# GpSimd takes one weight piece and half of a subtraction behind each norm, and the feed-forward's last transposes move between held products

## The chip, the cores and the metric

The kernel runs on one core of one Trainium2 chip. The metric is the device time of one execution in microseconds (us). The core has TensorE (PE, matrix products), VectorE (DVE, elementwise work), ScalarE (ACT, activations and copies), GpSimd (POOL, here elementwise work and loads of rows) and SyncE (SP, whose queue issues the weight loads). Each engine works its own instruction queue in order, and waits on semaphores of the others.

## The reference: what is computed

A first block (three token mixers and a mixture of experts) feeds a second block of four transformer layers over 256 tokens of width 1024. The change lies in the second block:

```python
def layer_norm(x, g, b):
    mu = xf.mean(-1, keepdims=True)
    var = jnp.square(xf - mu).mean(-1, keepdims=True)
    return (xf - mu) * lax.rsqrt(var + LN_EPS) * g + b

def swiglu(x, w_gate_up, w_down):
    gate, up = split(x @ w_gate_up)            # D_FF = 2816 each
    return (silu(gate) * up) @ w_down

for i in range(4):                             # attention kinds A, B, C, A
    h = mixer(x)
    x = layer_norm(DN_ALPHA * x + h, ln_g[i, 0], ln_b[i, 0])
    x = layer_norm(DN_ALPHA * x + swiglu(x, w_gate_up[i], w_down[i]), ln_g[i, 1], ln_b[i, 1])
```

All values are float32.

## The kernel before, in words

**Products.** Each float32 matrix is split into a high part (a cast to the type that PE reads, L240 for weights, L218 for activations, on ACT) and a low remainder (L242 and L219, a subtraction on DVE). A product is three matrix instructions: high x high, high x low, low x high (L254, L255, L256 in `mm3_steps`; L264, L265, L262 in `mm3_part`). The 256 tokens are two halves of 128 (t = 0, 1).

**Weight pieces.** `stream` cuts a weight matrix into pieces of 128x1024, two row blocks of 128 each; a projection over 1024 rows takes four of them. `unit` loads one piece (SP, into one of four raw buffers), casts it on ACT and subtracts on DVE, which frees the raw buffer for the next load. The split pair goes into one of three buffers of its own or, where `pair` names one, into one of four buffers that the attention heads use otherwise (`flat_heads`).

**Norms.** After each of the eight sublayers `finish` runs: the residual of half 0 (L1993 or L1995 with the statistics L1996), `normalise` of half 0, its transposes on PE (`turn`, L370) and the split of these (L218, L219), then the same for half 1. `normalise` takes mean and variance (L2011), the reciprocal root in seven steps on 128x1 (`rsqrt`, L326 to L341), the two halves of 512 columns of (y - mean) * g (L2014) and the two halves of y * r + b (L2016). All of it runs on DVE. The row vectors g and b are loaded by DMAs that POOL issues (L400).

**Behind a norm.** The first projection that follows (of the attention in `project_at` with `first`, of the feed-forward in `ffn` at u = 0) takes its four pieces as one group: all products of half 0, the high parts first, then `rest`, which turns half 1, then those of half 1. So PE has the work of half 0 while half 1 is normalised.

**End of the feed-forward.** `ffn` runs eleven steps of 256 hidden columns: gate and up products, SwiGLU (L2101 on ACT, L2103 on DVE), four transposes (L2117), their split, and one step later the down products into four accumulators, acc[t][n]. In the last step (u = 10) the down products of step 9 for half 0 are held back (`held`: two pieces, for n = 0 and n = 1, twelve products), then come the transposes of step 10, then the products of step 10 for half 0 (`last`), then all 24 of half 1, under which half 0 is normalised.

**What sets the order.** The kernel is traced in program order; a planner then orders each engine's queue by simulated times, and `after(ins)` keeps what it encloses behind `ins` on that engine. `self.order` carries the order of PE through the last products.

Of the kernel before, what the change touches and what calls it, by code (L numbers as in the profile page):

```python
# [9 lines left out]
F32 = mybir.dt.float32  # L10
# [4 lines left out]
ALU = mybir.AluOpType  # L15
AX = mybir.AxisListType
ACT, DVE, PE = mybir.EngineType.Activation, mybir.EngineType.DVE, mybir.EngineType.PE
P = 128
D = 1024
KT = D // P  # L20
D_FF = 2816
# [11 lines left out]
ONE, ALL = (1, 1, 1, 1), (4,)  # L33

# [115 lines left out]
class Core:  # L150


    def __init__(self, tc, I, ctx):
# [11 lines left out]
        self.behind = self.behind_act = None  # L165
# [61 lines left out]
    def unit(self, srcs, nk, pair=None, raw=None):  # L227


        nc = self.nc  # L230
        n = sum(x.shape[2] for x in srcs)
        view = lambda t: t[:, : nk * n].rearrange("p (k n) -> p k n", k=nk)
        raw = self.raw() if raw is None else raw
        h, l = self.split_pair() if pair is None else pair
        at = 0
        for x in srcs:
            nc.sync.dma_start(view(raw)[:, :, at : at + x.shape[2]], x)
            at += x.shape[2]
        with self.after(self.behind_act if pair is None else None):
            nc.scalar.copy(h[:, : nk * n], raw[:, : nk * n])  # L240
        with self.after(self.behind if pair is None else None):
            nc.vector.tensor_sub(l[:, : nk * n], raw[:, : nk * n], h[:, : nk * n].bitcast(F32))  # L242
        return view(h), view(l)
# [23 lines left out]
    def stream(self, w, cols, nk=KT, pair=lambda: None):  # L267

        v = w.rearrange("(k p) n -> p k n", p=P)
        for k in range(0, nk, 2):  # L270
            yield self.unit([v[:, k : k + 2, c : c + n] for c, n in cols], 2, pair())
# [1340 lines left out]
class Block2:  # L1612
# [52 lines left out]
    def project_at(self, first, xT, w, cols, pss):  # L1665

        c = self.c
        if first:
            pairs = chain([None] * self.first_pairs, (self.flat_heads() for _ in count()))
            self.first_pairs = 0  # L1670
            c.project(xT, c.stream(w, cols, pair=lambda: next(pairs)), pss, groups=ALL if self.rest else ONE, rest=self.rest)
# [334 lines left out]
    def normalise(self, y, st, rows):  # L2006
# [6 lines left out]
        for sl in HALVES:  # L2013
            nc.vector.scalar_tensor_tensor(y[:, sl], y[:, sl], mv[:, 0:1], rows[0][:, sl], ALU.subtract, ALU.mult)  # L2014
# [47 lines left out]
    def ffn(self, xT, i, x, more):  # L2062
# [19 lines left out]
        def add_all(t, ks):  # L2082

            for n in range(2):
# [6 lines left out]
        for u in range(nu):  # L2091
            pss = [c.mm() for _ in range(2)]
            units = c.stream(wg, [(256 * u, 256), (D_FF + 256 * u, 256)], pair=self.flat_heads)
# [11 lines left out]
            if u == nu - 1:  # L2105
                self.order = c.last(PE)
                held = list(pieces(*pend, lambda: next(pairs)))
                add_all(0, held)
# [6 lines left out]
            for kk in range(2):  # L2115
                for t in range(2):
                    nc.tensor.transpose(ps[:, kk * 256 + t * P : kk * 256 + (t + 1) * P], av[t][:, kk * P : (kk + 1) * P], c.ident)  # L2117
# [73 lines left out]
```

## Time and profile before

| | us |
|---|---|
| median of three runs (2033.51 to 2035.86) | 2034.7 |
| the profiled execution | 2037.31 |
| its span, first to last instruction | 2035.5 |
| PE busy | 1931.8 |
| DVE busy | 1336.6 |
| ACT busy | 1035.3 |
| POOL busy | 135.9 |

PE's granted clock over the span was 0.973 of full speed. Busy time is the union of an engine's instructions. In a timeline row, the bracket behind an instruction gives the idle time of its engine before it and what ended that. A row with x4 merges four like instructions that follow each other. Starts are in us from the span's start; the line is that of the kernel before.

### The profile page before, as it was taken

How to read it: one execution, taken by the hardware profiler on the slowest of the kernel's cores; microseconds unless marked ns; L12 is line 12 of the kernel's file. 1: busy time of each engine (PE TensorE's matmuls, PEld its weight loads, DVE VectorE, ACT ScalarE, POOL GpSimd, SP SyncE). 2: the span in 40 equal slices, each digit the busy share in tenths (PEclk: the TensorE clock that was granted, in tenths of full speed). 3: DMA queues.
4: the chain of work that ended last, by engine and by line, in shares of the span. 5: the costliest groups of instructions: out<-in, count | busy, mean ns of one | idle time of the engine just before them, and what ended most of it. 6: DMA issues, size and time to landing. Idle time of an engine off the chain costs nothing.

```text
span 2035.5 us, 27804 instructions
## 1 busy us (share of the span) xinstructions
PE 1931.8 (95%) x10012; PEld 1546.8 (76%) x10012; DVE 1336.6 (66%) x2324; ACT 1035.3 (51%) x1656; POOL 135.9 (7%) x259
## 2 busy tenths in 40 slices
PE   6998998989998999999999999999999999999997
PEld 2886886867786678887888877887767888767886
DVE  4689887868897775556555466556566555867555
ACT  5555654546774744434655555443563444454442
POOL 2110000000002000002111200000110000300000
PEclk8999998989998899999999999999999999989999
DMA  9546644777995356654543456664554655435662
GB/s 310 162 140 194 183 139 147 236 247 245 321 323 162 116 166 199 186 176 131 170 136 110 147 178 202 191 186 145 156 176 129 201 187 176 155 104 175 188 189 80
DMA packets 272403, 364.61 MB, mean 179 GB/s; under 512 B 17018, under 2 KB 206677, under 8 KB 272256
## 3 DMA queue, kind: packets, MB, share of 16 engines
q1 hardware_dynamic: 264832, 338.38, 52.5%
q0 software_dynamic: 7424, 24.36, 3.8%
q8 instruction: 81, 1.33, 0.3%
q14 instruction: 66, 0.54, 0.1%
HBM read 359.53 MB, written 3.15 MB: 178 GB/s over the span
## 4 chain that ended last, share of the span: by engine, by line
PE 59%; DVE 6%; ACT 2%; DMA 1%; issue 1%; POOL 0%; SPq 0%; DVEq 0%; ACTq 0%; POOLq 0%
PE mm L254 14%; PE mm L255 13%; PE mm L256 13%; PE acc L254 4%; PE acc L256 4%; PE acc L255 4%; PE acc L1752 1%; PE acc L1650 1%; DVE arena L242 1%; PE acc L1929 1%; PE acc L2117 1%; ACT arena L240 1%; DVE arena L2014 1%; PE acc L1749 1%; DMA arena<-in_w_gate_up 1%; PE acc L1925 1%
## 5 line engine op out<-in xcount | busy, mean ns | idle before, releaser
L242 DVE TENSOR_TENSOR arena<-arena,arena 128x1024 fp32r<-128x1024 f32 x597 | 716.9, 1213 | 480.6 <-ACT arena L240 475.8
L240 ACT CAST arena<-arena 128x1024 fp32r<-128x1024 f32 x597 | 614.0, 1039 | 549.4 <-PE mm L256 298.9
L254 PE MATMUL mm<-arena 128*128 128x512 f32 (+1 forms) x1856 | 703.3, 385 | 12.7 <-ACT arena L240 6.8
L255 PE MATMUL mm<-arena 128*128 128x512 f32 (+1 forms) x1856 | 706.0, 381 | 0.3 <-DVE arena L242 0.3
L256 PE MATMUL mm<-arena 128*128 128x512 f32 (+1 forms) x1856 | 698.7, 380 | 3.5 <-DVE arena L1386 1.3
L254 PEld LDWEIGHTS mm<-arena 128*128 128x128 f32 x1856 | 352.9, 191 | 85.8 <-ACT arena L240 8.3
L256 PEld LDWEIGHTS mm<-arena 128*128 128x128 f32 x1856 | 352.3, 191 | 71.2 <-DVE arena L219 4.1
L255 PEld LDWEIGHTS mm<-arena 128*128 128x128 f32 x1856 | 354.0, 191 | 61.5 <-issue 1.8
L254 PE MATMUL acc<-arena 128*128 128x512 f32 (+5 forms) x736 | 235.5, 360 | 7.3 <-ACT arena L218 7.3
L255 PE MATMUL acc<-arena 128*128 128x512 f32 (+5 forms) x736 | 235.4, 351 | 0.5 <-DVE arena L219 0.5
L256 PE MATMUL acc<-arena 128*128 128x512 f32 (+4 forms) x736 | 231.8, 350 | 0.0
L218 ACT CAST arena<-acc 128x512 fp32r<-128x512 f32 (+2 forms) x174 | 92.7, 542 | 179.1 <-PE acc L2117 79.8
L219 DVE TENSOR_TENSOR arena<-acc,arena 128x512 fp32r<-128x512 f32 (+2 forms) x174 | 108.1, 632 | 99.1 <-ACT arena L218 98.7
L254 PEld LDWEIGHTS acc<-arena 128*128 128x128 f32 (+1 forms) x736 | 125.0, 190 | 40.3 <-issue 11.6
L255 PEld LDWEIGHTS acc<-arena 128*128 128x128 f32 (+1 forms) x736 | 125.7, 190 | 21.6 <-issue 1.8
L256 PEld LDWEIGHTS acc<-arena 128*128 128x128 f32 (+1 forms) x736 | 124.7, 190 | 20.5 <-DVE arena L219 1.7
L1685 ACT ACTIVATE arena<-arena,nm 128x128 f32<-128x128 f32 (+2 forms) x128 | 65.9, 517 | 27.1 <-DVE nm L1684 27.1
L768 DVE SCALAR_TENSOR_TENSOR arena<-arena 128x192 f32<-128x192 f32 (+1 forms) x160 | 64.9, 430 | 2.4 <-ACT arena L766 0.9
L1684 DVE CUSTOM_DVE_ANT_0 arena<-acc,arena 128x128 f32<-128x128 f32 (+2 forms) x128 | 53.1, 465 | 13.6 <-PE acc L256 13.6
L370 PE MATMUL acc<-arena 128*128 128x128 f32 x200 | 32.9, 302 | 24.1 <-DVE arena L1020 8.2
L370 PEld LDWEIGHTS acc<-arena 128*128 128x128 f32 x200 | 24.4, 153 | 34.8 <-DVE arena L1020 8.3
L2101 ACT ACTIVATE arena<-mm 128x256 f32<-128x256 f32 x88 | 32.4, 379 | 24.4 <-PE mm L256 11.9
(354 smaller groups left out, 1497.8 us busy)
## 6 DMA issues: line engine op xcount, KB each, us to landing
arena<-in_w_gate_up SPq DMA_DIRECT2D x352, 256.0 KB, 4.0
arena<-in_w_down SPq DMA_DIRECT2D x88, 512.0 KB, 3.6
arena<-in_b_w_qkv SPq DMA_DIRECT2D x144, 256.0 KB, 3.0
arena<-in_w_in SPq DMA_DIRECT2D x56, 512.0 KB, 4.0
arena<-in_ada_w SPq DMA_DIRECT2D x48, 512.0 KB, 5.7
arena<-in_moe_w_gate SPq DMA_DIRECT2D x64, 256.0 KB, 4.6
arena<-in_moe_w_up SPq DMA_DIRECT2D x64, 256.0 KB, 4.9
arena<-in_moe_w_down SPq DMA_DIRECT2D x32, 512.0 KB, 5.3
```

What stands on the lines that cost most here:

```text
L218: self.nc.scalar.copy(h, src)
L219: self.nc.vector.tensor_sub(l, src, h.bitcast(F32))
L240: nc.scalar.copy(h[:, : nk * n], raw[:, : nk * n])
L242: nc.vector.tensor_sub(l[:, : nk * n], raw[:, : nk * n], h[:, : nk * n].bitcast(F32))
L254: yield t.matmul(out, x[0], w[0], start=start, stop=False)
L255: yield t.matmul(out, x[0], w[1], start=False, stop=False)
L256: yield t.matmul(out, x[1], w[0], start=False, stop=stop)
L370: self.nc.tensor.transpose(ps[:, j * P : (j + 1) * P], src[:, j * P : (j + 1) * P], self.ident)
L768: nc.vector.scalar_tensor_tensor(ov[:, rows], x, w, ov[:, rows], ALU.mult, ALU.add)
L1684: nc.vector.tensor_tensor_reduce(pr, s, mask, -0.125, 3e38 if sink is None else sink, ALU.add, ALU.min, nm)
L1685: nc.scalar.activation(pr, pr, AF.Exp, bias=nm, scale=-1.0, accum_out=l)
L2101: nc.scalar.activation(s, ps[:, :256], AF.Silu)
```

## The change

In `unit`, pieces marked `pool` are copied and subtracted by POOL, with no order imposed; `stream` marks those whose number stands in `pool`. The first projection of each attention (`project_at`) and of each feed-forward (u = 0) marks piece 3, the fourth. In `normalise` the second half of (y - mean) * g becomes two POOL instructions, a subtraction with one value for each partition and a multiplication; the first half stays on DVE, which also keeps both last steps. In `ffn`, at the last step, the held products for n = 0 come first, then the transposes, then those for n = 1. The unused `behind_act` goes.

```diff
--- before.py
+++ after.py
@@ -31,6 +31,8 @@
 RAW, PAIRS, MM, PROBS, AHEAD = 4, 3, 3, 8, 2
 HALVES = slice(0, 512), slice(512, 1024)
 ONE, ALL = (1, 1, 1, 1), (4,)
+
+POOLED = (3,)
 
 
 def _parts_of_two_pi():
@@ -162,7 +164,7 @@
             t = self.const.tile([P, words], dt, name=f"arena{len(self.arenas)}")
             self.arenas[dt] = Arena(t, words, kept)
         self.raw(), self.split_pair()
-        self.behind = self.behind_act = None
+        self.behind = None
         self.row_bufs = 1
         self.nf = None
         self.ident = self.tile((P,), F32, "w", "ident")
@@ -224,7 +226,7 @@
     def split_pair(self):
         return self.parts((1024,), "w", "w", PAIRS)
 
-    def unit(self, srcs, nk, pair=None, raw=None):
+    def unit(self, srcs, nk, pair=None, raw=None, pool=False):
 
 
         nc = self.nc
@@ -236,8 +238,11 @@
         for x in srcs:
             nc.sync.dma_start(view(raw)[:, :, at : at + x.shape[2]], x)
             at += x.shape[2]
-        with self.after(self.behind_act if pair is None else None):
-            nc.scalar.copy(h[:, : nk * n], raw[:, : nk * n])
+        if pool:
+            nc.gpsimd.tensor_copy(h[:, : nk * n], raw[:, : nk * n])
+            nc.gpsimd.tensor_tensor(l[:, : nk * n], raw[:, : nk * n], h[:, : nk * n].bitcast(F32), ALU.subtract)
+            return view(h), view(l)
+        nc.scalar.copy(h[:, : nk * n], raw[:, : nk * n])
         with self.after(self.behind if pair is None else None):
             nc.vector.tensor_sub(l[:, : nk * n], raw[:, : nk * n], h[:, : nk * n].bitcast(F32))
         return view(h), view(l)
@@ -264,11 +269,11 @@
             t.matmul(out, x[0], w[0], start=start, stop=False)
             t.matmul(out, x[0], w[1], start=False, stop=False)
 
-    def stream(self, w, cols, nk=KT, pair=lambda: None):
+    def stream(self, w, cols, nk=KT, pair=lambda: None, pool=()):
 
         v = w.rearrange("(k p) n -> p k n", p=P)
         for k in range(0, nk, 2):
-            yield self.unit([v[:, k : k + 2, c : c + n] for c, n in cols], 2, pair())
+            yield self.unit([v[:, k : k + 2, c : c + n] for c, n in cols], 2, pair(), pool=k // 2 in pool)
 
     def last(self, engine=None):
         for i in reversed(self.nc.cur_bb.bb.instructions):
@@ -1668,7 +1673,7 @@
         if first:
             pairs = chain([None] * self.first_pairs, (self.flat_heads() for _ in count()))
             self.first_pairs = 0
-            c.project(xT, c.stream(w, cols, pair=lambda: next(pairs)), pss, groups=ALL if self.rest else ONE, rest=self.rest)
+            c.project(xT, c.stream(w, cols, pair=lambda: next(pairs), pool=POOLED), pss, groups=ALL if self.rest else ONE, rest=self.rest)
         else:
             c.project(xT, c.stream(w, cols), pss)
 
@@ -2010,8 +2015,10 @@
         r = c.sm.tile([P, 1], F32, tag="rstd", name="rstd")
         nc.vector.bn_aggr(mv, st)
         c.rsqrt(r, mv[:, 1:2], "rs1", 1.0, LN_EPS)
-        for sl in HALVES:
-            nc.vector.scalar_tensor_tensor(y[:, sl], y[:, sl], mv[:, 0:1], rows[0][:, sl], ALU.subtract, ALU.mult)
+        first, second = HALVES
+        nc.vector.scalar_tensor_tensor(y[:, first], y[:, first], mv[:, 0:1], rows[0][:, first], ALU.subtract, ALU.mult)
+        nc.gpsimd.tensor_scalar(y[:, second], y[:, second], mv[:, 0:1], None, ALU.subtract)
+        nc.gpsimd.tensor_tensor(y[:, second], y[:, second], rows[0][:, second], ALU.mult)
         for sl in HALVES:
             nc.vector.scalar_tensor_tensor(y[:, sl], y[:, sl], r, rows[1][:, sl], ALU.mult, ALU.add)
 
@@ -2079,9 +2086,9 @@
         def add(t, n, k, aT, w):
             c.mm3(acc[t][n], [a[:, t * P : (t + 1) * P] for a in aT], [x[:, 512 * n : 512 * n + 512] for x in w], k == 0, k == 2 * nu - 1)
 
-        def add_all(t, ks):
-
-            for n in range(2):
+        def add_all(t, ks, *halves):
+
+            for n in halves or range(2):
                 for k in ks:
                     with c.after(self.order):
                         add(t, n, *k)
@@ -2090,7 +2097,7 @@
         pairs = (f() for f in (lambda: None,) * 3 + (self.flat_heads,))
         for u in range(nu):
             pss = [c.mm() for _ in range(2)]
-            units = c.stream(wg, [(256 * u, 256), (D_FF + 256 * u, 256)], pair=self.flat_heads)
+            units = c.stream(wg, [(256 * u, 256), (D_FF + 256 * u, 256)], pair=self.flat_heads, pool=() if u else POOLED)
             if u:
                 c.project(xT, units, pss)
             else:
@@ -2105,16 +2112,20 @@
             if u == nu - 1:
                 self.order = c.last(PE)
                 held = list(pieces(*pend, lambda: next(pairs)))
-                add_all(0, held)
+                add_all(0, held, 0)
             elif pend is not None:
                 for k in pieces(*pend):
                     for t in range(2):
                         for n in range(2):
                             add(t, n, *k)
             ps = c.tr()
-            for kk in range(2):
-                for t in range(2):
-                    nc.tensor.transpose(ps[:, kk * 256 + t * P : kk * 256 + (t + 1) * P], av[t][:, kk * P : (kk + 1) * P], c.ident)
+            with c.after(self.order if u == nu - 1 else None):
+                for kk in range(2):
+                    for t in range(2):
+                        nc.tensor.transpose(ps[:, kk * 256 + t * P : kk * 256 + (t + 1) * P], av[t][:, kk * P : (kk + 1) * P], c.ident)
+            if u == nu - 1:
+                self.order = c.last(PE)
+                add_all(0, held, 1)
             aT = c.parts((512,), "xT", "T", 3)
             c.split(aT[0], aT[1], ps)
             aT = [a.rearrange("p (k t) -> p k t", k=2) for a in aT]
```

## Rows read from the trace of the kernel before

**Rows 1.** The page: busy us (share, instructions) by engine, the chain by engine.

```profile
PE 1931.8 (95%) x10012; PEld 1546.8 (76%) x10012; DVE 1336.6 (66%) x2324; ACT 1035.3 (51%) x1656; POOL 135.9 (7%) x259
...
PE 59%; DVE 6%; ACT 2%; DMA 1%; issue 1%; POOL 0%; SPq 0%; DVEq 0%; ACTq 0%; POOLq 0%
```

**Rows 2.** Timeline of PE: start, us, engine, line, operation, count [idle <-releaser].

```profile
721.69 0.50 PE L254 MATMUL mm<-arena 128*128 128x512 f32 x1 [0.37 <-DVE arena L1995]
...
909.25 0.50 PE L254 MATMUL acc<-arena 128*128 128x512 f32 x1 [0.68 <-ACT arena L218]
...
920.40 0.50 PE L264 MATMUL mm<-arena 128*128 128x512 f32 x1 [1.34 <-ACT arena L218]
...
1225.59 1.98 PE L262 MATMUL mm<-arena 128*128 128x512 f32 x8
...
1228.62 1.38 PE L370 MATMUL acc<-arena 128*128 128x128 f32 x8 [1.06 <-DVE arena L2016]
...
1828.83 0.50 PE L254 MATMUL mm<-arena 128*128 128x512 f32 x1 [1.15 <-DVE arena L1995]
```

**Rows 3.** Timeline of DVE: norm of half 1 ahead of layer 1's feed-forward.

```profile
1224.91 0.21 DVE L2011 BATCH_NORM_AGGREGATE mv<-bn 128x2 f32<-128x12 f32 x1
...
1225.22 1.41 DVE L2014 SCALAR_TENSOR_TENSOR arena<-arena,mv 128x512 f32<-128x512 f32 x2
...
1226.73 0.22 DVE L332 SCALAR_TENSOR_TENSOR rs<-rstd,rs 128x1 f32<-128x1 f32 x1
...
1227.82 1.42 DVE L2016 SCALAR_TENSOR_TENSOR arena<-arena,rstd 128x512 f32<-128x512 f32 x2
```

**Rows 4.** Timeline at the end of layer 0's feed-forward: transposes, cast, remainder.

```profile
907.98 0.60 PE L2117 MATMUL acc<-arena 128*128 128x128 f32 x4
...
908.62 0.59 ACT L218 CAST arena<-acc 128x512 fp32r<-128x512 f32 x1 [1.84 <-PE acc L2117]
...
909.23 0.69 DVE L219 TENSOR_TENSOR arena<-acc,arena 128x512 fp32r<-128x512 f32 x1 [1.20 <-ACT arena L218]
```

**Rows 5.** Timeline of ACT and DVE behind it, ahead of layer 1.

```profile
915.98 3.90 ACT L240 CAST arena<-arena 128x1024 fp32r<-128x1024 f32 x4 [6.77 <-PE acc L256]
919.77 1.06 ACT L218 CAST arena<-acc 128x512 fp32r<-128x512 f32 x2
...
919.90 1.23 DVE L242 TENSOR_TENSOR arena<-arena,arena 128x1024 fp32r<-128x1024 f32 x1 [0.22 <-ACT arena L240]
```

**Rows 6.** Single lines over the span: count, duration in ns min/median/max, starts, forms.

```profile
L1635 POOL TENSOR_TENSOR arena<-arena x44: 317/462/1502, 644.8 to 1776.2; 128x128 f32<-128x128 f32 x40, 128x64 f32<-128x64 f32 x4
...
L1787 POOL COPY arena<-arena x4: 613/624/1495, 648.7 to 1755.0; 128x512 f32<-128x512 f32 x4
...
L1738 DVE TENSOR_TENSOR l<-l,es x16: 151/160/280, 668.8 to 1817.1; 128x4 f32<-128x4 f32 x16
```

**Rows 7.** Timeline of POOL and DVE side by side, three stretches.

```profile
668.62 0.46 POOL L1635 TENSOR_TENSOR arena<-arena 128x128 f32<-128x128 f32 x1 [9.64 <-DVE es L1736]
668.82 0.28 DVE L1738 TENSOR_TENSOR l<-l,es 128x4 f32<-128x4 f32 x1 [0.27 <-ACT es L1737]
...
1452.46 1.23 DVE L242 TENSOR_TENSOR arena<-arena,arena 128x1024 fp32r<-128x1024 f32 x1 [2.49 <-ACT arena L240]
1452.51 1.50 POOL L1637 TENSOR_TENSOR arena<-arena 128x128 f32<-128x128 f32 x1
...
1762.57 0.45 POOL L1636 TENSOR_TENSOR arena<-arena 128x128 f32<-128x128 f32 x1
1762.58 1.53 DVE L242 TENSOR_TENSOR arena<-arena,arena 128x1024 fp32r<-128x1024 f32 x1
```

**Rows 8.** Timeline of PE and DVE ahead of layer 3's feed-forward.

```profile
1826.84 0.84 PE L256 MATMUL mm<-arena 128*128 128x512 f32 x3
1826.95 1.23 DVE L242 TENSOR_TENSOR arena<-arena,arena 128x1024 fp32r<-128x1024 f32 x1 [4.33 <-ACT arena L240]
1828.09 1.28 DVE L1995 TENSOR_TENSOR arena<-arena,mm 128x512 f32<-128x512 f32 x2
1829.29 1.28 DVE L1996 BATCH_NORM_STATS2 bn<-arena 128x6 f32<-128x512 f32 x2
```

## The prediction

> **What bounds the kernel now.** I read the page's busy line first: TensorE (PE) is busy for 95% of the span, VectorE (DVE) for 66%, GpSimd (POOL) for 7% [rows 1]. The chain that ended last gives PE 59% and DVE 6% [rows 1], so the total is PE's work plus the places where PE stands still, and only these can be won. So I next took PE's timeline and kept the instructions with idle time before them [rows 2]. They lie round the eight places where a token half is normalised. Four are the ends of a feed-forward, where PE waits for ScalarE's (ACT's) cast of the last transposes (0.68 us). At the three ends that lead to a further layer PE waits again for ACT (1.34 us at the first). Before each feed-forward PE waits for the second half's norm (1.06 us in layer 1), and in layers 0 and 3 also for the residual (0.37 and 1.15 us). Third, DVE's timeline through one norm shows what such a wait is made of [rows 3]: mean and variance are there at 1225.12 (1224.91 + 0.21), two subtract-and-scale steps take 1.41 us, seven tiny steps for the reciprocal root follow, and the first of the two last steps starts at 1227.82, 2.70 us after the mean. Each half step takes about 0.70 us of DVE (1.41 / 2).
>
> **Part 1: the last transposes between held products.** Now the four transposes run after all twelve held products, at 907.98, ACT's cast starts at 908.62 when they are done, and PE restarts at 909.25 [rows 2, 4]. In the new order six held products stand behind the transposes. Twelve products and the transposes are unchanged in number, so PE's work is the same; six products at just under 0.25 us each (eight in 1.98 [rows 2]) are 1.4 us, and the cast (0.59) and the remainder's subtraction (0.69) need 1.3 us one after the other [rows 4]. So the 0.68 us idle goes, and so does a smaller wait for the remainder, which is there at 909.92 when the third product is due at about 909.7 (909.25 + 2 x 0.24): 0.9 us at each of four ends, **-3.7 us**. What is late next is nothing on PE: the first held half covers the SwiGLU product that feeds the transposes. All four ends count, the last one too, since DVE's final norms start from PE's last products there.
>
> **Part 2: the fourth weight piece on GpSimd.** It takes one cast (0.98 us, 3.90 / 4 [rows 5]) from ACT and one subtraction (1.23 us) from DVE at eight places, and adds a copy and a subtraction of 128x1024 on POOL. POOL's copy of 128x512 takes 0.62 us, its two-input step 0.317 us on 64 columns and 0.46 on 128 [rows 6]; that is 2.1 ns a column over 0.18 us, so 128x1024 is about 2.4 us, and the copy at most 1.2 (twice 0.62): with a hand-over some 3.7 us against 2.2 on ACT and DVE. Where does it pay? Ahead of layers 1 and 2 the fourth cast stands last of four in ACT's queue (915.98 to 919.88), the cast of the transposes waits behind it until 919.77, and DVE does its subtraction at 919.90, in front of the rest of the second half's norm [rows 5]. Off both queues, the transposes' cast can follow the third cast, at 918.9 (915.98 + 3 x 3.90 / 4), and DVE saves 1.23 plus the idle 0.22 ahead of it, 1.4 us. The piece's buffer is the one that PE reads last, so POOL can start when the fourth cast could, about 918.0, and its products come twelve products (2.9 us) after PE restarts at about 919.6: 4.5 us for 3.7, covered. Two such places: **-2.9 us**. In layer 3's feed-forward the fourth piece lands late: its subtraction at 1826.95 stands in front of two residual steps whose first input was long ready, and PE waits 1.15 us for them [rows 2, 8]. Without it the first residual and its statistics are over early and the second starts when PE's products end (1827.68, from 1826.84 + 0.84), so one residual and one statistics step later, 1.4 us, the statistics are done, at 1829.1 and not at 1830.57 (1829.29 + 1.28): **-1.5 us**. Layer 0 has the same shape with a wait of 0.37 us, so between 0.4 and 1.5; I take **-0.7**, nearer to its own row. Ahead of layer 3's attention the order of the pieces is another and I see no gain; in layers 1 and 2's feed-forward the piece is split long before it is wanted: nothing, as PE's attention and output products cover it. On entry to the second block POOL is slower by 1.5 us (3.7 - 2.2) on work that PE wants soon: between 0 and +1.5, I take **+0.5**. Behind the new waits on POOL stand only row loads with long lead and, in layer 1, the rotary steps. Sum of part 2: -4.6 us.
>
> **Part 3: half of the mean's subtraction on GpSimd.** DVE gives up one of two 0.70 us steps in each of 16 norms; POOL gets a tensor_scalar and a multiplication on 128x512 (0.18 + 512 x 2.1 ns = 1.27 us). The tensor_scalar is nowhere in the trace: from 0.62 us (the copy) to 1.27 (the two-input step). Were the engines independent, POOL would be done 2.1 us after the mean (0.1 + 0.62 + 0.1 + 1.27), DVE would want its half at 2.70 (2.70 less one step, plus the first of the last two), and the norm would be shorter by 0.70. But they are not [rows 7]. POOL's 0.46 us step started 0.05 us behind a DVE step that reads two tensors and took 1.50, ending 0.32 us after the DVE step. The other way round, the same DVE step took 1.53 instead of 1.23 with POOL in front of it. Even a DVE step of four columns took 0.28 us instead of 0.16 beside POOL, ending with it [rows 6, 7]. Whoever asks first keeps the other out until its reading is over (for DVE, about 0.15 us before POOL's recorded end). The tiny steps of the reciprocal root read two operands each, so they are caught as well.
>
> The Trainium skill states this as a rule that speaks against the change (SBUF — State Buffer, Who interferes with whom): a vector instruction with two SBUF inputs and a GpSimd instruction that reads SBUF exclude each other for a whole instruction. The rows agree (1.50 against 0.46 us), and by the rule the sum is the one that follows.
>
> So I lay the norm out again, in us after the mean. DVE's remaining subtract step runs 0.1 to 0.85. POOL's tensor_scalar, which starts at about the same time and loses, ends at 0.85 + 0.62 - 0.14 = 1.33 (0.14 of its own start passes while it is shut out: 0.46 - 0.32 [rows 7]). The first two-input tiny step, L332, is due at 0.95 (1226.73 is 1.61 after the mean, less 0.66 for the step that left) and runs at 1.2 to 1.4. POOL's multiplication starts at 1.4 and reads until about 2.5; the next or next but one tiny step waits until then. From L332 to the last steps DVE needs 1.09 us (1227.82 - 1226.73 [rows 3]), of which 0.65 to 0.85 are left, so the last steps start at 3.17 to 3.37 instead of 2.70: **+0.5 to +0.65**. If POOL wins the first race it comes to +0.62. With 1.27 for the tensor_scalar the delay is about +1.1. I take 0.6 per norm, nearest the copy, which like the tensor_scalar reads one tensor. The very last step doesn't wait for POOL, which is done by 2.7, while DVE comes to it at 3.9.
>
> The Trainium skill (GPSIMD Engine Reference, Engine selection) says that one-input work on GpSimd runs at roughly line rate; by that the delay would be the lower one. No run shown here has the operation.
>
> Both norms of a place count: before the feed-forwards PE's products end just as the first half's last step does, so a longer first norm moves the transposes and all DVE work behind them, and the second norm is then waited for outright [rows 2, 3]. 16 x 0.6 = **+9.6 us**.
>
> **Sum.** -3.7 - 4.6 + 9.6 = **+1.3 us**. The profiled execution took 2037.3 us (span 2035.5), 2.6 above the median of three runs, 2034.7; differences carry over, so 2034.7 + 1.3 = **2036.0 us**. About 0.2% (4 us) is what a measurement of this kernel can tell from no change, so this is "the same". Each 0.1 us in the norm's delay is worth 1.6 us.
>
> **Rivals.**
> *The port does not bind in the norm* (POOL starts late enough, or the tiny steps slip through). Then each norm is shorter by up to 0.70. The first norm's share is mostly hidden, since PE's products end at the same moment, so some 8 of 16 count fully: -8.3 - 5.6 = about -14, **2021 us**. Rows 7 speak against it; for it only that no row shows a tensor_scalar on POOL.
> *GpSimd holds VectorE up for longer* (the slower side): the tensor_scalar costs near 1.27 us, so the tiny steps are shut out twice for longer, at DVE's first two-input tiny step and again at the multiplication. With +1.0 per norm the sum is 16 - 8.3 = +7.7, **2042 us**; with 1.2 it is 2045.6. It decides from a delay of 0.77 per norm on (12.3 - 8.3 = 4.0). For it: a step of 0.46 us became 1.50 in rows 7, and POOL's new steps are longer; against it: the copy's 0.62.
> *The planner places things otherwise*: residual steps or the POOL pieces in another order, or the piece kept ahead of a norm's subtraction in POOL's queue, where it costs up to 3.7 us. Then part 2 gives between nothing (+4.6 against my sum, **2041**) and somewhat more than I count (**2030**).
>
> **How the numbers follow.** Forecast with its own range (delay 0.4 to 0.8 per norm, -1.9 to +4.5: 2033 to 2039): 0.50. Port not binding: 0.17. GpSimd slow: 0.25. Planner: 0.08. Faster by over 0.2%: 0.06 (the forecast's tail) + 0.17 + 0.05 (planner) = 0.28. Within: 0.36 + 0.05 (GpSimd slow, but little) = 0.41. Slower: 0.08 + 0.20 + 0.03 = 0.31. The range that leaves out about 2 in 10 reaches from half way into the first rival, 2026, to 2044, between the second rival's two values.
>
> **What the profile after would show.** Part 1: no idle before PE's first product behind the last cast, and transposes with products of six on both sides. Part 2: one cast fewer ahead of the transposes' cast, PE back about 0.8 us earlier after the first norm; POOL's copy about 1.2 us, its subtraction 2.4, no PE wait on POOL. Part 3: the step from the mean to the first last step at 3.2 to 3.4 us instead of 2.70, tiny steps of 0.16 us stretched to 1 us beside POOL's multiplication. I am wrong if that step is below 2.7 (first rival), or above 3.5 (second), or if PE's 0.68 us waits stay.

## The result and the profile after

The changed kernel took 2047.6 us in the median of six runs (2038.1 to 2053.9), the kernel before 2034.3 on the same chip: a ratio of 1.0063 (95% interval 1.0042 to 1.0083), 0.6% slower. The forecast was 2036.0, its range ended at 2044.

The profiled execution of after is the shortest of the six: 2038.12 us with a span of 2036.3, so 0.8 longer than the profiled one of before. Its page, busy time and the chain that ended last:

```profile
PE 1918.1 (94%) x10012; PEld 1542.3 (76%) x10012; DVE 1327.0 (65%) x2300; ACT 1026.5 (50%) x1648; POOL 228.8 (11%) x307
...
PE 28%; issue 28%; DVE 4%; POOL 4%; DMA 2%; ACT 1%; POOLq 0%; SPq 0%; DVEq 0%; ACTq 0%
```

Against [rows 1], POOL works 93 us more and stands on the chain with 4%, where it had 0. The norm of half 1 ahead of layer 1's feed-forward, the one of [rows 3], in the timelines of DVE and POOL (start, us, engine, line, operation; in brackets the idle time ahead and what ended it):

```profile
1222.71 0.21 DVE L2016 BATCH_NORM_AGGREGATE mv<-bn 128x2 f32<-128x12 f32 x1
...
1223.02 2.10 POOL L2020 TENSOR_SCALAR arena<-arena,mv 128x512 f32<-128x512 f32 x1 [4.97 <-DVE mv L2016]
1223.03 0.74 DVE L2019 SCALAR_TENSOR_TENSOR arena<-arena,mv 128x512 f32<-128x512 f32 x1
...
1223.87 0.39 DVE L337 SCALAR_TENSOR_TENSOR rs<-rstd,rs 128x1 f32<-128x1 f32 x1
1224.29 0.16 DVE L343 SCALAR_TENSOR_TENSOR rs<-rs 128x1 f32<-128x1 f32 x1
...
1225.12 0.75 DVE L2023 SCALAR_TENSOR_TENSOR arena<-arena,rstd 128x512 f32<-128x512 f32 x1
1225.20 1.80 POOL L2021 TENSOR_TENSOR arena<-arena 128x512 f32<-128x512 f32 x1
1227.04 0.75 DVE L2023 SCALAR_TENSOR_TENSOR arena<-arena,rstd 128x512 f32<-128x512 f32 x1 [1.16 <-POOL arena L2021]
```

The mean is there at 1222.92. Of the two last steps (L2023, one for each half of the columns) the first starts 2.20 us after it; before it was 2.70. But POOL needs 2.10 us for the subtraction and 1.80 for the multiplication, and the second of the two waits 1.16 us for it: it starts 4.12 us after the mean, where before, with the two in a row, it started at 3.37 (2.70 and one step of 0.67). So the first column half of a norm is 0.50 us earlier and the second 0.75 later. PE transposes both column halves, and in place of the one wait of 1.06 us in [rows 2] it has three in that place (timeline of PE, instructions with idle time ahead):

```profile
1218.99 0.63 PE L375 MATMUL acc<-arena 128*128 128x128 f32 x4 [0.84 <-DVE arena L2023]
...
1225.93 0.66 PE L375 MATMUL acc<-arena 128*128 128x128 f32 x4 [0.84 <-DVE arena L2023]
...
1227.93 0.63 PE L375 MATMUL acc<-arena 128*128 128x128 f32 x4 [1.34 <-DVE arena L2023]
```

At the entry to the second block, POOL's and PE's timelines:

```profile
628.11 1.05 POOL L242 CAST arena<-arena 128x1024 fp32r<-128x1024 f32 x1
629.10 0.54 POOL L405 DMA_DIRECT2D arena<-in_mask_c  x1
633.79 0.54 POOL L1770 DMA_DIRECT2D arena<-in_a_sinks  x1 [4.16 <-DVE arena L1774]
634.34 2.36 POOL L243 TENSOR_TENSOR arena<-arena,arena 128x1024 fp32r<-128x1024 f32 x1
...
636.75 0.80 PE L270 MATMUL mm<-arena 128*128 128x512 f32 x1 [3.52 <-POOL arena L243]
```

The planner put two row loads between the piece's copy and its subtraction; the second waits 4.16 us for DVE, and PE stands 3.52 us for the subtraction behind it. At the end, POOL's DRAIN instructions of the program's last line (duration in ns, shortest/median/longest; first and last start), in after and then in before:

```profile
L2198 POOLq DRAIN  x3: 50/113/8701, 2026.8 to 2036.1; - x3
...
L2187 POOLq DRAIN  x3: 51/113/7439, 1840.8 to 2035.2; - x3
```

In after POOL's queue drains for 8.70 us from 2026.8 on, to 2035.5, 4 us behind SyncE, whose queue writes the output and whose own DRAIN stands at 2031.5. The last mean to the end of the span takes 11.80 us; before it took 7.13.

How far a kernel is behind the one before at the end of a norm's statistics (us, from the profiled executions; s is a second half; the last row adds the stretch to the end of the span):

| place, time before | after | part 1 | parts 1, 2 | part 1, layers 1 and 2 | part 3 |
|---|---|---|---|---|---|
| layer 0 attention, 723.7 | +0.3 | -0.4 | +5.3 | -2.7 | -0.2 |
| the same, s, 731.9 | +1.1 | -0.4 | +5.2 | -2.7 | +0.5 |
| layer 0 feed-forward, 914.2 | +0.1 | -1.6 | +4.1 | -3.9 | +2.3 |
| the same, s, 923.9 | +0.1 | -1.6 | +2.6 | -5.3 | +2.8 |
| layer 1 attention, s, 1225.1 | -2.2 | -4.8 | -0.5 | -8.7 | +4.2 |
| layer 1 feed-forward, s, 1417.1 | -3.1 | -6.0 | -3.2 | -11.3 | +4.9 |
| layer 2 feed-forward, s, 1738.9 | -3.7 | -5.7 | -4.4 | -11.9 | +8.1 |
| layer 3 attention, 1830.8 | -4.3 | -11.7 | -3.8 | -16.6 | +7.1 |
| the last, s, 2028.4 | -3.9 | -12.9 | -5.0 | -17.9 | +8.8 |
| end of the span | +0.8 | -12.9 | -5.0 | -17.9 | +13.4 |

The first row holds mostly the first block, where nothing was changed and executions differ by some us: of the +5.3 of parts 1, 2 in it, 4.4 are there before the second block starts (at 631.7 us, in before at 627.3). One profiled execution of after was hardly longer than one of before; the medians differ by 13. The rest lies between executions. For each run its span and mean granted clock are known. Span times clock is what the span would be at PE's full clock ("granted"); the rest, span times (1 - clock), is what the level of 1.2 GHz took ("lost"; not exact, for an idle PE at that level loses nothing). The six runs of after lie at clocks from 0.976 to 0.968, and the time follows: the shortest lost 49 us, the longest 66. The kernel before spread over 2.4 us beside it, and over 7 to 15 in the larger sets below.

### The profile page after: what moved, and what is told of

The parts are those of the page before. It is cut to its first block, busy times and chain, and to the rows that moved or that the text cites. A ratio compares the mean times of both kernels' runs of the same rounds, so it can differ in the third digit from the quotient of the medians.

```text
span 2036.3 us, 27826 instructions
## 1 busy us (share of the span) xinstructions
PE 1918.1 (94%) x10012; PEld 1542.3 (76%) x10012; DVE 1327.0 (65%) x2300; ACT 1026.5 (50%) x1648; POOL 228.8 (11%) x307
## 3 DMA queue, kind: packets, MB, share of 16 engines
q8 instruction: 81, 1.33, 0.3%
## 4 chain that ended last, share of the span: by engine, by line
PE 28%; issue 28%; DVE 4%; POOL 4%; DMA 2%; ACT 1%; POOLq 0%; SPq 0%; DVEq 0%; ACTq 0%
PE mm L259 7%; PE mm L260 7%; PE mm L261 7%; POOL arena L2020 2%; PE acc L259 1%; POOL arena L2021 1%; PE acc L260 1%; PE acc L261 1%; PE acc L1655 1%; DVE arena L247 1%; DMA arena<-in_w_gate_up 1%; ACT arena L245 1%; PE acc L1934 1%; DMA arena<-in_b_w_o 1%; POOL arena L243 1%
## 5 line engine op out<-in xcount | busy, mean ns | idle before, releaser
L247 DVE TENSOR_TENSOR arena<-arena,arena 128x1024 fp32r<-128x1024 f32 x589 | 706.1, 1210 | 473.9 <-ACT arena L245 467.3
L245 ACT CAST arena<-arena 128x1024 fp32r<-128x1024 f32 x589 | 606.1, 1039 | 555.7 <-PE mm L261 288.9
L259 PEld LDWEIGHTS acc<-arena 128*128 128x128 f32 (+1 forms) x736 | 124.4, 188 | 36.2 <-issue 10.1
L260 PEld LDWEIGHTS acc<-arena 128*128 128x128 f32 (+1 forms) x736 | 125.2, 188 | 21.5 <-issue 2.2
L2020 POOL TENSOR_SCALAR arena<-arena,mv 128x512 f32<-128x512 f32 x16 | 33.6, 2098 | 613.6 <-DVE mv L2016 613.6
```

The source lines that it names most:

```text
L259: yield t.matmul(out, x[0], w[0], start=start, stop=False)
L260: yield t.matmul(out, x[0], w[1], start=False, stop=False)
L2020: nc.gpsimd.tensor_scalar(y[:, second], y[:, second], mv[:, 0:1], None, ALU.subtract)
```

## The experiments

All kernels but the first are compared with runs of the kernel before on the same chip; granted and lost are means over the runs.

| kernel | median us | before | ratio (95%) | granted | lost |
|---|---|---|---|---|---|
| before (63 runs) | | | | 1981 | 50 |
| after, first six runs | 2047.6 | 2034.3 | 1.0063 (1.0042 to 1.0083) | 1988 | 57 |
| again: after | 2046.1 | 2031.4 | 1.0072 (1.0049 to 1.0095) | 1986 | 58 |
| p1: part 1 | 2021.7 | 2031.4 | 0.9946 (0.9932 to 0.9959) | 1976 | 44 |
| p12: parts 1, 2 | 2028.5 | 2031.4 | 0.9976 (0.9961 to 0.9990) | 1978 | 48 |
| p3: part 3 | 2052.9 | 2031.4 | 1.0103 (1.0086 to 1.0119) | 1989 | 62 |
| best: 1, 2, no entry | 2029.3 | 2032.1 | 0.9993 (0.9977 to 1.0009) | 1974 | 55 |
| fix: best and part 3 but at the end | 2039.4 | 2032.1 | 1.0026 (1.0010 to 1.0041) | 1982 | 56 |
| p3q: a quarter on POOL | 2035.2 | 2032.1 | 1.0011 (0.9996 to 1.0026) | 1983 | 51 |
| late: one more DVE step | 2046.1 | 2032.1 | 1.0066 (1.0043 to 1.0089) | 1991 | 54 |
| p1b: part 1 | 2021.8 | 2033.6 | 0.9950 (0.9932 to 0.9968) | 1975 | 47 |
| a12: part 1, layers 1, 2 | 2020.8 | 2033.6 | 0.9933 (0.9919 to 0.9948) | 1973 | 46 |
| top: a12, second pieces | 2020.3 | 2033.6 | 0.9925 (0.9906 to 0.9943) | 1971 | 46 |
| tail: after, last norms on DVE | 2038.8 | 2033.6 | 1.0037 (1.0016 to 1.0057) | 1984 | 54 |

The theories: A, several small prices (the second of the two last steps, which the expectations call the second last step, the entry, the drain) and PE's clock, which falls behind the waits that they make. B, GpSimd's work in the norms holds VectorE up, and that is the whole loss. C, the fourth piece on GpSimd makes PE wait and its clock fall.

**The changed kernel again.** No edit.

> The changed kernel once more. Its first six times spread from 2038 to 2054 us while the kernel before stays within 2.4 us, and its clock over the span falls from 0.976 to 0.968 with the time. Theory A (several small prices, and TensorE's clock): each execution pays 4 to 5 us on entry (PE stands 3.5 us on GpSimd's remainder of the fourth piece) and about 4 us at the end (GpSimd's DRAIN of 8.7 us); the rest differs from run to run with the time TensorE spends at 1.2 GHz. Then the median is again 2045 to 2050, and a profiled execution slower than 2038 shows the same waits and more time at half clock (98 us in the first one), 2 us of it for each us lost. Theory B (GpSimd holds VectorE up for longer, the prediction's second rival): the same median, but a slower execution shows longer waits round the norms and the same time at half clock.

2046.1 us, and the same waits: 3.42 us for POOL at the entry, 0.95 and 1.20 at a second half. Behind the latter the clock fell, in this execution in layer 3 (PE's timeline, then three stretches with busy us of PE, PEld, DVE, ACT and POOL, each with its count, and the granted clock behind them):

```profile
1840.65 0.63 PE L375 MATMUL acc<-arena 128*128 128x128 f32 x4 [0.95 <-DVE arena L2023]
1842.47 1.09 PE L375 MATMUL acc<-arena 128*128 128x128 f32 x4 [1.20 <-DVE arena L2023]
...
1844.22 0.63 PE L261 MATMUL mm<-arena 128*128 128x512 f32 x1
...
1846.41 0.39 PE L261 MATMUL mm<-arena 128*128 128x512 f32 x1
```

```profile
1839.00:1842.40 3.40, 1.33 (x8) 0.66 (x6) 2.10 (x7) 0.97 (x2) 3.02 (x3) 1.00 0.00 0
1842.50:1845.90 3.40, 3.40 (x10) 2.85 (x11) 1.54 (x3) 0.59 (x1) 0.07 (x1) 0.51 0.43 154
1846.00:1849.40 3.40, 3.40 (x17) 2.80 (x16) 2.02 (x2) 2.63 (x3) 0.00 (x0) 1.00 0.00 0
```

PE stood twice, for 0.95 and 1.20 us; then it ran at 1.2 GHz for 3.4 us, where ten matmuls took the time of 17 behind it: 1.4 us lost for one fall. It fell in the same way at 736.6; in the first profile of after, with the same waits (0.93 and 1.19, 0.95 and 1.19), it did not at either place. So these waits are the same from run to run, and the clock behind them is not.

**Parts alone.** p1 leaves the pieces and the norm as before, p3 the pieces and the transposes, p12 the norm. The line of the pieces, in p1 and p3:

```diff
-POOLED = (3,)
+POOLED = ()
...
```

> Part 1 alone: the transposes between held products; no GpSimd work is added. Both theories: the 0.68 us idle at four ends goes, and a little more, 0.9 to 1.1 us at each end, so 2030 to 2031 us against 2034.3, with a spread of 2 to 3 us as before. If the spread of the changed kernel came from part 1, this kernel would show it too: single times over 2038.

> Parts 1 and 2: the mean's subtraction stays on VectorE whole. Theory A: part 1 gives 3.7 us, part 2 gives 2.9 to 5 us ahead of the layers and loses 4 to 5 us on entry, and there is no DRAIN of some us at the end: 2029 to 2033 us, with a small spread. Theory B: part 3 is the whole loss, so the prediction's sum for the other two holds, 2026 to 2027 us. Theory C (the fourth piece on GpSimd makes PE wait and its clock fall): 2040 us or more, spread over more than 6 us.

> Part 3 alone: half of the mean's subtraction on GpSimd. Theory A: the second half of each norm's last step is 0.75 us later, which counts at four to six places (3 to 5 us), and GpSimd's DRAIN at the end costs 4 us: 2041 to 2044 us. Theory B: nearly the whole loss and the spread, 2045 to 2050 us. Theory C (the loss is the fourth piece's): 2034 to 2038 us.

Part 1 gains 9.7 us, not 3.7; both theories were off there. Part 2 on top of it loses 6.7 us by the medians (2028.5 against 2021.7). p12 lies between A's and B's figures, but its eleven runs spread over 16.7 us (2019.5 to 2036.2), where A had expected a small spread and C one of over 6. Part 3 alone loses 21.5: more than the whole change, and above what both A and B expected, with B nearer. But its trace shows A's places: DVE's steps in the norm are those of after, with the last step of the second column half 0.75 late, and the last mean to the end takes 11.80 us.

**Is it GpSimd, or the lateness?** p3q gives POOL 256 columns and DVE 768, and leaves the last two norms on DVE (else it is p3); late is the kernel before, without POOL, with one DVE step more in each norm (y = max(y, y)):

```diff
-        first, second = HALVES
+        first, second = slice(0, 768), slice(768, 1024)
```

```diff
         for sl in HALVES:
+            if sl.start:
+                nc.vector.scalar_tensor_tensor(y[:, sl], y[:, sl], 1.0, y[:, sl], ALU.mult, ALU.max)
             nc.vector.scalar_tensor_tensor(y[:, sl], y[:, sl], r, rows[1][:, sl], ALU.mult, ALU.add)
```

> Part 3 alone with half of its size: VectorE subtracts 768 columns, GpSimd 256, and the last feed-forward's norms stay on VectorE. Theory A (part 3 costs through the second last step, which waits for GpSimd, and through the DRAIN): GpSimd now needs some 2 us after the mean in place of 4.0, the second last step no longer waits, VectorE saves 0.3 us a norm, and there is no DRAIN at the end: 2027 to 2033 us, with the clock of the kernel before (0.975 to 0.977). Theory B (any GpSimd work in the norm holds VectorE up by the shared port): at least 0.3 us later in each of 14 norms, 2037 us or more.

> The kernel before, with one more VectorE step of 128x512 (0.7 us, which leaves the values as they are) ahead of the second last step of each of the 16 norms; nothing is put on GpSimd. It makes the second half of each norm as late as part 3 does (0.75 us) and leaves GpSimd and its DRAIN out. Theory A (lateness, and what it does to the clock, is the price): 4 to 6 us of waits and the clock down to 0.971 to 0.973, 2038 to 2046 us. If the clock falls only where GpSimd works: at most 2037 us at the clock of before.

p3q's norm, same place:

```profile
1224.53 1.72 POOL L2021 TENSOR_SCALAR arena<-arena,mv 128x256 f32<-128x256 f32 x1 [5.65 <-DVE mv L2016]
1224.53 1.01 DVE L2020 SCALAR_TENSOR_TENSOR arena<-arena,mv 128x768 f32<-128x768 f32 x1
...
1226.33 0.77 POOL L2022 TENSOR_TENSOR arena<-arena 128x256 f32<-128x256 f32 x1
1226.54 0.58 DVE L346 SCALAR_TENSOR_TENSOR rstd<-rs,rstd 128x1 f32<-128x1 f32 x1
1227.15 1.41 DVE L2027 SCALAR_TENSOR_TENSOR arena<-arena,rstd 128x512 f32<-128x512 f32 x2
```

POOL is done at 1227.10, and both last steps run in a row from 1227.15 on, 2.72 us after the mean (1224.43), as before (2.70); the time is that of before within 0.3%, 2035.2 us, which neither A (2027 to 2033) nor B (2037 or more) had forecast. So GpSimd in the norm costs little as long as it is not what ends last, and gains nothing either: the 0.40 us that DVE saves (1.01 for 1.41) is given back at L346, held for 0.42 us by POOL's multiplication. In late the planner put the added step ahead of the tiny steps, not between the last two, so both column halves are 0.54 later (the last steps start 3.24 us after the mean): a delay like part 3's in size, not the same one. With POOL as before it costs 14 us by the medians: 9.1 of granted time, where 16 x 0.54 gives 8.6, and 4.6 of lost clock. That speaks for A and against B: a norm that ends later is dear without GpSimd too.

**Without the entry and the drain.** best leaves the piece on entry on ACT and DVE; fix is after with that and with the last two norms on DVE; tail is after with the latter alone (`more` is false in the last feed-forward only). The edits, cut to the parts of the lines that differ and, in the second, to one of two calls:

```diff
-c.stream(w, cols, pair=lambda: next(pairs), pool=POOLED)
+c.stream(w, cols, pair=lambda: next(pairs), pool=() if entry else POOLED)
```

```diff
-        self.normalise(ys[0], st[0], rows)
+        self.normalise(ys[0], st[0], rows, more)
```

> Parts 1 and 2 without the piece on entry: there the fourth piece stays on ScalarE and VectorE, since GpSimd's remainder stood behind a row load that waited 4.16 us for VectorE, and PE stood 3.5 us for it. Theory A: 4 to 5 us less than parts 1 and 2 with it, whose median was 2028.5, so 2022 to 2025 us; against part 1 alone (2021.7) that is the same or up to 3 us less. Theory C (GpSimd's piece makes PE wait at the other seven places too): 2027 us or more.

> All three parts, without GpSimd's piece on entry and with the last feed-forward's two norms on VectorE, so that GpSimd's last work lies some 180 us before the end. Theory A: 4.65 us less for the DRAIN, 4 to 5 less on entry, against 2046 to 2047.5: 2036 to 2039 us; what is left over parts 1 and 2 is the later last step of each norm and the clock. Theory B (the work on GpSimd inside the norms is the whole loss): 2043 us or more.

> The changed kernel with the two norms of the last feed-forward on VectorE, as before; all else is as changed. It takes GpSimd's last work from 2027 to some 1840 us, so its DRAIN (8.7 us) is over long before the end. Theory A: 4.65 us less than the changed kernel (2046 to 2047.5), so 2041 to 2043 us, and the stretch from the last statistics to the end is 7.1 us, not 11.8. If the DRAIN only stands beside another wait of the same length (the output's DMA): the same time as the changed kernel, and 11.8 us again.

The drain is confirmed. In tail POOL's long DRAIN starts at 1843.9:

```profile
L2202 POOLq DRAIN  x3: 50/112/7506, 1843.9 to 2034.7; - x3
```

The stretch from the last mean to the end is 7.15 us again (11.80 in after), and the means of the last two norms lie 7.0 us apart, as before, not 7.8: 5.4 us in all. The ratio fell by 0.26 to 0.35%, 5 to 7 us.

best against fix is part 3 in 14 of the 16 norms, without the drain: 10 us by the medians, 7.4 of them granted.

The entry was a miss for A, and the median lies where C had put it. Granted time fell by 3.8 us against p12, as A expected, but the lost part rose by 7 and the median did not move (2029.3 and 2028.5, on two chips). In best PE reaches the residuals of layers 0 and 3 earlier and waits there; behind both waits the clock fell, at 722.6 and 1821.7:

```profile
722.08 0.50 PE L259 MATMUL mm<-arena 128*128 128x512 f32 x1 [3.43 <-DVE arena L2001]
...
1820.89 0.50 PE L259 MATMUL mm<-arena 128*128 128x512 f32 x1 [2.35 <-DVE arena L2001]
```

**What part 2 is worth where it was counted.** a12 is part 1 with the fourth piece on POOL in the attention of layers 1 and 2 only (first two lines of the diff, which has the ends of lines alone; its feed-forwards have none); top adds the second piece of each feed-forward, not the fourth (the last two); p1b is p1 beside them.

```diff
-pool=POOLED)
+pool=POOLED if self.layer in (1, 2) else ())
...
-pool=() if u else POOLED)
+pool=() if u else (1,))
```

> Part 1 alone again, beside the next three. It was 2021.7 us against 2031.4, a ratio of 0.9946, where four ends of 0.9 us should give 3.7 us. If the other 6 us are the clock and waits that follow from it, the ratio is again 0.993 to 0.997, and the profile again shows no PE wait of 0.68 us behind the last cast, while the number of falls of the clock differs from the first profile. If the first six times were luck, the ratio is 0.998.

> Part 1, and of part 2 only the two places where the prediction counted 1.4 us each: the fourth piece of the attention of layers 1 and 2. Nothing of the feed-forwards, the entry or layer 3 is on GpSimd. If the step of the prediction holds, 2.0 to 2.9 us less than part 1 alone at the same clock: the statistics of the second half ahead of layers 1 and 2 end 1.4 us earlier each. If GpSimd's piece costs clock wherever it stands, the time is that of part 1 or more.

> As the one with layers 1 and 2, and in each feed-forward the second piece on GpSimd, not the fourth. In the trace of the kernel before, the piece that lands late ahead of the residual of layers 0 and 3 is the second one by the order of the loads; the prediction took it for the fourth. If that was the fault, PE's waits for the residual (0.37 and 1.15 us before, 1.1 and 2.5 in the changed kernel) go in both layers, 1.0 to 1.9 us less than the one with layers 1 and 2 alone. If GpSimd holds the residual up in another way (the port, a later load), these waits stay over 0.3 and 1.0 us.

a12 gains what the prediction said. Its statistics of the second half come 1.47 and 1.46 us earlier ahead of layers 1 and 2 (table: -3.9 to -5.3 there), granted time is 2.8 us under p1b's, and PE's wait of 1.34 us is 0.39:

```profile
914.18 1.20 POOL L242 CAST arena<-arena 128x1024 fp32r<-128x1024 f32 x1 [180.04 <-PE acc L261]
915.47 2.40 POOL L243 TENSOR_TENSOR arena<-arena,arena 128x1024 fp32r<-128x1024 f32 x1
...
915.59 0.50 PE L269 MATMUL mm<-arena 128*128 128x512 f32 x1 [0.39 <-ACT arena L220]
```

By the medians the gain over p1b is 1.0 us, less than the intervals of the two tell apart. So C does not hold for these two pieces. top decides little: PE's waits for the residual in layers 0 and 3 are 0.33 us each, but in a12 they are 0.62 and 0.33 already. At 2020.3 us (0.9925) it is faster than both kernels; so are p1, p1b and a12, and the four are not told apart.

## Why the prediction was wrong, step by step

Put on one after the other on one chip, the parts are, by the medians: part 1 -9.7 us, part 2 on top of it +6.7, part 3 on top of both +17.6, together +14.7 (2046.1 against 2031.4). The forecast had -3.7, -4.6 and +9.6, together +1.3.

**Part 3, +9.6 by the prediction, failed in its second column half.** The race at the start went as laid out: the tensor_scalar lost to DVE's step. But it was priced at 0.62 us, nearest the copy. Its 2.10 us beside a DVE step of 0.74, and 1.72 at half the width beside 1.01, leave about 1.4 and 0.8 us of its own if DVE keeps it out for all but 0.08 of its step: an estimate, 2.5 ns a column, near the two-input step and over the upper bound of 1.27. (That step's rows, 0.317 us on 64 columns and 0.462 on 128, give 2.3 ns a column, not 2.1; this is small beside the rest.) So it ended 2.20 us after the mean, not 1.33. The multiplication then met not the tiny steps but the first of the two last steps, lost again, and ended at 4.08 instead of 2.5. Two sentences fell with that: the first of the two last steps came at 2.20, not at 3.2 to 3.4, with tiny steps of 0.16 (only the first two-input one was longer, 0.39 where it took 0.22 before); and "the very last step doesn't wait for POOL" was wrong by 0.75 us in each norm. By the prediction's own sign a start below 2.70 spoke for its first rival, 2021 us: the sign looked at the wrong one of the two steps. In the profiled execution of part 3 alone 0.7 to 0.8 us are lost between the norms of the two token halves ahead of each feed-forward, and 0.5 to 0.8 at the feed-forwards' ends. That 14 norms without the drain come to 10 us (best against fix), close to +9.6, is luck: the delay sits at another step.

The Trainium skill (SBUF — State Buffer, Who interferes with whom) has the two engines exclude each other for a whole instruction. The 2.10 against 0.74 us and the 0.58 us of L346 agree with it; the steps of 0.16 us in the midst of POOL's tensor_scalar do not. The other page cited in the prediction (GPSIMD Engine Reference, Engine selection: one-input work at roughly line rate) does not hold for this operation here, with the 2.5 ns a column of the estimate against 1.2 for the copy.

**The drain, no term at all.** The end of the program was never looked at. POOL's queue takes 6.9 us from the end of its last instruction (2028.60) to the end of the DRAIN (2035.47). In before it did too, from 1841.4 to 1848.2, hidden 187 us ahead of the end. Part 3 moved POOL's last work to 2028.6: +4.67 us (11.80 less 7.13 from the last mean to the end).

**Part 2, -4.6 by the prediction, +6.7 measured.** Four steps:

- The 2 x 1.4 us ahead of layers 1 and 2 hold (1.47 and 1.46).
- At the entry I took +0.5 and asked what stands behind POOL's new work, not what the planner can put into the middle of it: a row load, already in the queue of before, that waits for DVE. PE's products there end up 5.3 us later (from the first transposes to the first product of half 1 it takes 15.4 us, before 10.1). Most of it comes back in the same layer, where two waits, 1.13 and 0.96 us before, are 0.47 and 0.32, and where after loses 5.0 us to the lower level and before 7.6. From these transposes to the first mean of the layer the profiled executions with the piece on POOL take 96.2 to 98.0 us (after, again, p12, tail) and the ten without it 94.8 to 97.7. So the 3.5 us wait was missed, and that +0.5 is not far from what is left of it is luck.
- In layer 3 I put a change of order at nothing in the sum (it stands among the rivals). The order that part 1 has there by itself (below) is gone in p12, best and after: from the last mean of layer 2 to the next one the ten profiled executions without it take 91.0 to 92.8 us and the four with it 85.9 to 87.2, which is most of the +6.7. a12 and top have the order, so the pieces of layers 1 and 2 do not cost it; which of the others does, no run separates.
- Ahead of the feed-forwards of layers 3 and 0 (-1.5 and -0.7) I took the piece that lands late in [rows 8] for the fourth, by its place as the last in time. It is the second. In after the fourth is split early on POOL and the late one still stands in front of the residual; in top, where POOL has the second, POOL's is the late one (POOL, ACT, DVE and PE ahead of layer 3's feed-forward in after, then POOL in top):

```profile
1809.93 1.04 POOL L242 CAST arena<-arena 128x1024 fp32r<-128x1024 f32 x1 [34.92 <-DMA arena<-in_w_gate_up]
...
1821.59 1.05 ACT L245 CAST arena<-arena 128x1024 fp32r<-128x1024 f32 x1 [4.20 <-DMA arena<-in_w_gate_up]
1822.67 1.23 DVE L247 TENSOR_TENSOR arena<-arena,arena 128x1024 fp32r<-128x1024 f32 x1 [4.82 <-ACT arena L245]
1823.81 1.28 DVE L2000 TENSOR_TENSOR arena<-arena,mm 128x512 f32<-128x512 f32 x2
1824.55 0.50 PE L259 MATMUL mm<-arena 128*128 128x512 f32 x1 [1.64 <-DVE arena L2000]
...
1810.42 1.04 POOL L242 CAST arena<-arena 128x1024 fp32r<-128x1024 f32 x1 [42.20 <-DMA arena<-in_w_gate_up]
```

The waits of 0.37 and 1.15 us grew to 1.18 and 1.64. In layer 0 the wait is 1.07 to 3.43 us in all six profiled executions with the feed-forwards' fourth piece on POOL (after, again, p12, best, fix, tail), and 0.33 to 0.62 in the eight others. So the growth goes with that piece, as C said; how it makes the wait longer was not settled. In best (3.43 and 2.35) PE arrives earlier and the late piece does not: from the entry PE is there after 91.8 us, in p12 after 94.0, and the piece's cast starts after 92.3 in both. So what was gained ahead is waited out.

**Part 1, -3.7 by the prediction, -9.7 and -11.8 measured.** The mechanism holds: the 0.68 us waits are gone in every kernel with part 1 and stand in the four without it (before, p3, p3q, late), and each end gains 1.2 us in p1's trace (-0.4 to -1.6 in the table), 4.8 in all, not 3.7: the term was 0.3 short at each end. The other 5 to 6 us come from a place that the edit does not touch. From layer 3's attention on, and before it nowhere but at the ends themselves, the planner orders the queues of PE, DVE and ACT differently, and a wait of 1.71 us for DVE's softmax steps at 1787.7 and the 1.15 us for the residual behind it become 0.35 and 0.33 (PE in before, then twice in p1):

```profile
1787.71 1.07 PE L1749 MATMUL acc<-arena 128*128 128x128 f32 x6 [1.71 <-DVE arena L1688]
...
1779.54 0.55 PE L1754 MATMUL acc<-arena 128*128 128x128 f32 x3 [0.35 <-DVE arena L221]
...
1817.18 0.50 PE L259 MATMUL mm<-arena 128*128 128x512 f32 x1 [0.33 <-DVE arena L2000]
```

The clock has a share: in this stretch before loses 6.8 us to the lower level, p1 none and the other three 1.7 to 3.4. p1b, a12 and top have this order and gain 5 to 6 us there; p12 and after do not (1.71 us again), so within the change part 1 is worth some 4 to 5.

**The clock, no term.** After loses some 58 us to the lower level where before loses 50; the drain's stretch, with an idle PE at half clock, holds 2.3 of that. I had taken differences between single executions to carry over to the median. Here they do not: the profiled one lost 49 us. Five of the extra falls stand some 4 us or less behind the start of a pair of PE waits of 0.9 to 1.4 us for a second half (736.6 and 1842.5 in again; 738.0, 932.6 and 1427.5 in p3), and best's two behind one long wait (3.43 and 2.35 us). Why the clock falls at such a place in one execution and not in another no run shows.

**The rivals.** The forecast's sign was slower by 1.3, within the noise. The second rival (2042 to 2045.6, GpSimd slow) came nearest in time and priced the tensor_scalar better ("near 1.27"), but did not have the mechanism: DVE's tiny steps were hardly shut out, and its very last step waited for POOL's result. The third (the planner places things otherwise) is what befell part 2, at the entry and in layer 3, but it let part 2 fall back to nothing at worst, where it came to +6.7.

The sum as it is now, on one chip, granted and lost: part 1 -4.3 and -5.3 (p1), part 2 +1.8 and +3.4 (p12 against p1), part 3 with the drain +8.3 and +10.8 (again against p12), together +5.8 granted and +8.9 lost. That is the 14.7 us of the medians there; more than half of it is the clock, for which the prediction had no term.

## What to carry to other kernels

Work handed to an idle engine has to be followed to its last instruction and its last reader: here 3.9 us of GpSimd replaced 0.7 us of VectorE, and the step that needed the result moved from 3.37 to 4.12 us after the mean. When an engine gets work near the end of a program for the first time, read what its queue still does after its last instruction, and when a planner orders the queues, identify a piece by a mark of its own, such as the engine that a trial run gives it, and not by its place in time, and expect the order to change in places that the edit does not touch. Where single runs of one kernel spread by up to 23.5 us (tail), compare medians and the granted clock of every run before explaining a single trace.

## What the runs showed of the hardware that I had not expected

GpSimd's DRAIN takes 6.9 us past its last instruction, after a row load (before) as after a multiplication (after), and the program ends only behind it. A GpSimd tensor_scalar with one value per partition costs about as much a column as a two-input step (1.72 us for 256 columns, 2.10 for 512, both beside a DVE step), not as the copy, by the estimate above. A GpSimd multiplication held a VectorE step of 128x1 for 0.42 us; a GpSimd tensor_scalar, once under way, held the first such step for 0.17 us (0.39 for 0.22) and those behind it not at all. And the same PE wait of 1.65 us in layer 3's attention was followed by a fall to 1.2 GHz in before (at 1779.0) and in p1b (at 1770.3), and by none in p1, which is the same kernel as p1b.
